# Low parts on VectorE, and weight sums beside the output projection, in the MLP of a two-layer hybrid encoder

## The chip, the cores and the metric

One core of one Trainium2 chip runs the whole program. The time is that of one execution on the device in microseconds; the number that stands for a kernel is the median of several executions. The profile is of one execution, whose own time is given beside its span.

Five engines work side by side: PE multiplies matrices and accumulates in PSUM, DVE, ACT and POOL work element by element, SP issues most DMA transfers. Each runs its own list of instructions in order, and waits where an operand is not there yet or a buffer is not free yet.

## The reference

A trunk of two layers on x of 1024 positions by 1024 features, all in float32. Layer 0 mixes by chunked attention, layer 1 by a gated DeltaNet; each is followed by the same kind of MLP, which is what the change touches.

```python
def rmsnorm(x, w):
    return x * rsqrt(mean(x * x, axis=-1) + EPS) * w

def squared_relu_mlp(h, w_up, w_down):          # w_up 1024 x 4096, w_down 4096 x 1024
    return jnp.square(jax.nn.relu(h @ w_up)) @ w_down

for i in range(2):
    x = x + mixer_i(rmsnorm(x, mixer_norm_i))   # attention, then DeltaNet; each ends in a projection w_o
    x = x + squared_relu_mlp(rmsnorm(x, mlp_norm[i]), w_up[i], w_down[i])
return rmsnorm(x, final_norm)
```

## The kernel before

**Precision.** A float32 product is made of three matmuls in a shorter format: high·high, high·low and low·high. The high part of an operand is a copy in that format (`high`, L1018, on ACT); the low part is the operand less its high part (`low`, L1011: on POOL by L1013 if the argument `pool` is set, else on DVE by L1015). So whatever is multiplied needs one operation on ACT and one on DVE or POOL first.

**Blocks.** After each mixer comes a block: its output projection (`out_proj`, L962), the up projection (`up`, L1149), the down projection. Activations lie transposed: features along the partitions, the 1024 positions in two halves of 512, called h = 0 and 1. The up projection is done in 16 units of 256 outputs, n = 0 to 15. A unit is a 2 x 2 block product by a scheme with seven products in place of eight: `block_product` (L1003) is one of the seven, 12 matmuls of 128 x 128 by 128 x 512. The scheme multiplies sums of the operands' blocks:

- sums of activations t1, t2, t3, t4, made once per block. `prep_up` (L473) makes them tile by tile as the output projection delivers x (L506, L511, L514 for the last four tiles). `finish` (in it) splits each of the sixteen tiles into high and low with `put`, sums the squares over the features on PE (the column sums, L333, of `ssum`, which L427 adds up), takes the reciprocal root on DVE in small steps (`inv_rms2`, L294 to L308, ending in `ry`), and spreads it over the partitions with PE (`row_bcast`, L347) and ACT (L349) into R.
- sums of weights S1, S2, S3 and s4, made for each unit. `up_weights` (L1031) loads two raw panels (L1036, buffers `wraw`, two of them in turn), makes four sums on POOL (L1021, L1024; the fourth is written over a quarter of the raw panel) and splits all into high and low. The first panel's parts are called w0, the second's w1; the second raw buffer comes free for the next unit's load when the low part of w1 is made. `first_up_weights` (L1108) does the same for unit 0, in buffers of its own, beside the output projection.

**Results of a unit.** A unit's products are added on DVE (L1161, L1198), scaled by R (L1163) and squared through a relu on ACT (L1164). `combine` (L1074) makes from them the sums that the down projection multiplies, four differences `c` of 128 x 512 per unit (`sub`, by `psub` on POOL), splits them (high on ACT, low on DVE at L1086) and stores them with SP (`gt<-c`, L1087). The down projection loads them again; L1458 adds its first products to x.

**Order.** The code around the change is written in the order of each engine's list: nothing is moved by a scheduler on PE, DVE, ACT and POOL, and SP's transfers follow. Generators give the steps: `out_proj` steps `weights` (which is `first_up_weights`) once for every tile of the projection, (m, h) in the order of L962, and `finish` at its end; `up` steps `finish`, and `more` and `rest` (which are `up_weights` of the next unit) between the products. In unit 0 the products come in the order: A11, A12 (added to the first on DVE), s4·22, s2·t2, s1·t1, s3·t3, 22·t4. In the later units they come as A11, s1·t1, s2·t2, A12, s3·t3, s4·22, 22·t4.

Of the kernel before, what the change touches and what calls it, by code (L numbers as in the profile page):

```python
# [12 lines left out]
ALU = mybir.AluOpType  # L13
# [195 lines left out]
class Trunk:  # L209
# [263 lines left out]
    def prep_up(self, xs, which, pool, xpool, spill):  # L473
# [44 lines left out]
        def put(t, j, pool):  # L518
            hi, lo = ops[t][j]
            self.high(hi, diffs[t][j])  # L520
            self.low(lo, diffs[t][j], hi, pool)

        def finish():
            hp = self.hi_lo()
            for t, (b, h) in {"t2": (0, 0), "t1": (4, 0), "t3": (0, 1), "t4": (4, 1)}.items():
                ops[t] = [hp[b + j][h] for j in range(4)]
            put("t2", 0, True)
            put("t2", 1, True)
            yield
            put("t2", 2, True)  # L530
            put("t1", 0, True)
            yield
            put("t2", 3, False)
            for j in range(1, 4):
                put("t1", j, True)
            yield
            r = self.inv_rms2(sums)
            next(r)
            for j in range(4):
                put("t3", j, j == 3)  # L540
                next(r, None)
                next(r, None)
            yield
            for j in range(4):
                put("t4", j, j > 1)
                next(r, None)
                next(r, None)
            for _ in r:
                pass
            yield  # L550
            R = self.new_R()
            for h in range(2):
                self.row_bcast(self.got[:, 4 * h : 4 * h + 4], R[:, h * HB : (h + 1) * HB], (self.aux, self.sqt)[h])
            yield R

        return ops, tile_done, finish()
# [405 lines left out]
    def out_proj(self, w, rhs, xs, done, finish, weights):  # L962
# [11 lines left out]
        for m, h in order:  # L974
            if h == 0 and m in self.started:
                ps = self.started[m][0]
            else:
                ps = self.bank()
                self.products(ps, *panels[m], rhs, h)
            if m < KT - 1:  # L980
                beside(2 + (m in (1, 2)))
            elif h == 0:
                beside(2)
            nc.vector.tensor_tensor(
                xs[m][:, h * HB : (h + 1) * HB], ps, xs[m][:, h * HB : (h + 1) * HB], ALU.add)
            if h == 0 and 2 <= m + 1 < KT:
                panels[m + 1] = self.load_w(w[m + 1])
            if (m, h) == (KT - 2, 1):
                beside(2)
            if (m, h) == (KT - 1, 0):  # L990
                last = done(m)
                next(last)
                beside(8)
            elif h == 1 and m < KT - 1:
                todo.append(done(m))
            next(weights, None)
        next(finish)
        next(last)
# [32 lines left out]
    def up_weights(self, i, n, ap, A):  # L1031
# [17 lines left out]
        self.padd(S1, a21, a22)  # L1049
        self.psub(S2, S1, a11)  # L1050
        yield

# [6 lines left out]
        self.high(A["s2"][0], S2)  # L1059
        self.psub(S3, a11, a21)  # L1060
        self.psub(a21, a12, S2)
        yield
# [11 lines left out]
    def combine(self, n, g, mp, gt):  # L1074
# [4 lines left out]
        def sub(z, x, y):  # L1079
            self.psub(t[z][:, HB:], x, y)  # L1080

# [25 lines left out]

    def first_up_weights(self, i, ap, ex, A):  # L1108

# [30 lines left out]
        self.low(A["s3"][1], S3, A["s3"][0], True)  # L1140
        for _ in range(5):
            yield
        w1 = [self.wp.tile([P, KT, P], F32R, name=self.nm("w" + z), tag="w" + z) for z in ("hi", "lo")]
        A["s4"], A["22"] = ([z[:, 4 * m : 4 * m + 4] for z in w1] for m in range(2))
        self.high(w1[0], raw[1])
        self.low(w1[1], raw[1], w1[0], True)
        yield

    def up(self, i, ops, ap, mp, pp, gr, gt, finish, A, tail):  # L1149

# [18 lines left out]
        for n in range(last + 1):  # L1169
            nxt, more = {}, iter(())  # L1170
            if n < last:
                more = self.up_weights(i, n + 1, ap, nxt)
# [29 lines left out]
            if n == 0:  # L1202
                next(finish)
                self.block_product(X, A["12"], ops["21"], True, True)
                add("p1", X)
                next(more)
                V = self.bank()
                self.block_product(V, A["s4"], ops["22"], True, True)
                next(finish)
                self.block_product(Y, A["s2"], ops["t2"], False, False)  # L1210
                copied("u2", Y)
                add("u2", V)
                next(more)
                self.block_product(Z, A["s1"], ops["t1"], True, True)
                copied("z5", Z)
                add("u2", Z)
                next(finish)
                next(more)
                self.block_product(Y, A["s3"], ops["t3"], False, False)
                add("z5", Y)  # L1220
                R = next(finish)
                next(more)
# [333 lines left out]
    def block(self, i, rhs, x, w, which, after, done=None, ahead=iter(()), norm=None):  # L1556
# [5 lines left out]
        with tc.tile_pool(name=f"xa{i}", bufs=1) as xa, tc.tile_pool(name=f"xb{i}", bufs=1) as xb, \  # L1562
# [7 lines left out]
            A = {}  # L1570
            first = self.first_up_weights(i, hx, ex, A)
            B = [{n: [None, None] for n in NAMES} for _ in range(2)]
# [21 lines left out]
            with tc.manual_schedule(engines=ENG):  # L1594
                self.out_proj(w, rhs, xs, tile_done, finish, first)
                sums = self.up(i, ops, hx, xp, yz, gr, gt, finish, A, end)
                next(end)
                self.down(i, hx, yz, got["xs"], chain(sums, late()), gr, gt, B, (got["A"], got["rest"]),
                          after, ahead, norm)
                if done:  # L1600
                    done(got["xs"])
# [996 lines left out]
```

## Time and profile before

| | |
|---|---|
| median of 3 runs | 2604.25 us (2602.82 to 2606.19) |
| the profiled execution | 2604.42 us |
| its span in the profile | 2602.0 us |
| mean granted clock of PE | 0.98 |
| first unit of block 0 | 563.87 to 595.38 us |
| units 1 to 14 of block 0 | from 595.38 us |
| first unit of block 1 | from 1939.42 us |

Every row of the profile names the line of the kernel, the engine, the operation, and what is written from what (`xs<-x,xs`). In a timeline a row begins with its start and its length in us; `x4` says that four like instructions follow each other; the bracket gives the idle time of the engine ahead of the row and what ended it. In a list of waits the three numbers are us in total, how often, and the longest. Names: `xs` are parts of activations (high, or low where DVE or POOL subtracts), `whi`, `wlo` the parts of raw weights, `ahi`, `alo` those of the sums of weights, `acc`, `y`, `z` accumulators in PSUM, `nt` copies of such accumulators.

### The profile page before, as it was taken

How to read it: one execution, taken by the hardware profiler on the slowest of the kernel's cores; microseconds unless marked ns; L12 is line 12 of the kernel's file. 1: busy time of each engine (PE TensorE's matmuls, PEld its weight loads, DVE VectorE, ACT ScalarE, POOL GpSimd, SP SyncE). 2: the span in 40 equal slices, each digit the busy share in tenths (PEclk: the TensorE clock that was granted, in tenths of full speed). 3: DMA queues.
4: the chain of work that ended last, by engine and by line, in shares of the span. 5: the costliest groups of instructions: out<-in, count | busy, mean ns of one | idle time of the engine just before them, and what ended most of it. 6: DMA issues, size and time to landing. Idle time of an engine off the chain costs nothing.

```text
span 2602.0 us, 36727 instructions
## 1 busy us (share of the span) xinstructions
PE 2476.6 (95%) x12638; PEld 2070.1 (80%) x12638; DVE 1925.0 (74%) x3275; ACT 1211.0 (47%) x2269; POOL 1336.2 (51%) x1112
## 2 busy tenths in 40 slices
PE   8999999999999899998888999999898999899997
PEld 6888888777888678886677788888787888688885
DVE  6665656777778778878578976675678787787887
ACT  6666667544555423234673334333335555533333
POOL 2444356536676656565464333332316666565656
PEclk9999999999999999999998999999999999999998
DMA  4222224315555876743443121123324555876642
GB/s 159 67 68 78 62 85 144 132 69 194 207 206 213 316 252 203 230 146 108 115 140 106 54 81 60 58 83 114 106 89 163 203 217 206 304 266 218 217 164 81
DMA packets 189049, 389.27 MB, mean 150 GB/s; under 512 B 54512, under 2 KB 61104, under 8 KB 188864
## 3 DMA queue, kind: packets, MB, share of 16 engines
q1 hardware_dynamic: 172592, 353.36, 40.5%
q10 hardware_dynamic: 16272, 33.58, 3.3%
q8 instruction: 99, 1.62, 0.3%
q14 instruction: 86, 0.70, 0.1%
HBM read 251.96 MB, written 126.52 MB: 145 GB/s over the span
## 4 chain that ended last, share of the span: by engine, by line
PE 59%; DVE 11%; DMA 4%; issue 3%; POOL 2%; ACT 1%; SPq 0%; DVEq 0%; ACTq 0%; POOLq 0%
PE y L1009 24%; PE z L1009 11%; PE acc L164 8%; PE acc L1009 6%; PE tp L164 3%; PE s L164 3%; DVE ft L164 2%; PE acc L280 1%; PE acc L279 1%; PE acc L278 1%; DVE fz L164 1%; DVE xs L394 1%; DMA wraw<-in_w_down_dram 1%; DVE x L1458 1%; DMA wraw<-in_w_up_dram 1%
## 5 line engine op out<-in xcount | busy, mean ns | idle before, releaser
L164 PE MATMUL acc<-xs,whi 128*128 128x512 f32 x1808 | 631.7, 413 | 8.4 <-DVE xp L164 5.2
L164 PEld LDWEIGHTS acc<-xs,whi 128*128 128x128 f32 x1808 | 333.5, 191 | 57.7 <-DVE xp L164 5.4
L164 PE MATMUL acc<-xs,wlo 128*128 128x512 f32 x896 | 368.6, 411 | 3.1 <-POOL wlo L164 3.1
L1009 PE MATMUL y<-xs,whi 128*128 128x512 f32 x1008 | 311.1, 390 | 3.5 <-DVE ssum L1161 3.5
L164 POOL TENSOR_TENSOR wlo<-wraw,whi 128x512 fp32r<-128x512 f32 x126 | 167.7, 1331 | 245.5 <-ACT whi L164 197.0
L1015 DVE TENSOR_TENSOR wlo<-wraw,whi 128x512 fp32r<-128x512 f32 (+1 forms) x180 | 202.2, 1124 | 40.1 <-ACT whi L1018 40.1
L1009 PEld LDWEIGHTS y<-xs,whi 128*128 128x128 f32 x1008 | 189.2, 188 | 43.7 <-DVE ssum L1161 4.3
L1009 PE MATMUL y<-xs,a 128*128 128x512 f32 x732 | 192.7, 400 | 23.4 <-DVE x L1458 23.3
L1024 POOL TENSOR_TENSOR s<-wraw 128x256 f32<-128x256 f32 (+1 forms) x93 | 91.9, 989 | 235.9 <-DVE a L1015 181.4
L1018 ACT ACTIVATE whi<-wraw 128x512 fp32r<-128x512 f32 (+2 forms) x191 | 146.5, 767 | 133.8 <-PE y L1009 86.1
L1009 PE MATMUL y<-xs,wlo 128*128 128x512 f32 x504 | 196.3, 389 | 0.0
L1458 DVE TENSOR_TENSOR x<-y,x 128x512 f32<-128x512 f32 x240 | 165.3, 689 | 41.1 <-PE y L1009 26.1
L1018 ACT ACTIVATE a<-s 128x256 fp32r<-128x256 f32 x122 | 63.9, 524 | 282.0 <-PE y L1009 166.5
L164 PEld LDWEIGHTS acc<-xs,wlo 128*128 128x128 f32 x896 | 171.7, 192 | 28.6 <-POOL wlo L164 4.3
L1009 PEld LDWEIGHTS y<-xs,a 128*128 128x128 f32 x732 | 139.3, 192 | 57.0 <-DVE x L1458 25.7
L1086 DVE TENSOR_TENSOR c<-c 128x512 fp32r<-128x512 f32 x128 | 151.9, 1206 | 35.7 <-POOL c L1021 34.5
L1009 PE MATMUL y<-xs,ahi 128*128 128x512 f32 x512 | 158.9, 391 | 6.1 <-DVE xs L1015 4.1
L1009 PE MATMUL acc<-xs,whi 128*128 128x512 f32 x528 | 163.6, 391 | 0.0
L164 POOL TENSOR_SCALAR pr<-pr,rs 128x640 f32<-128x640 f32 (+4 forms) x128 | 88.1, 692 | 129.3 <-DVE rs L164 96.7
L1009 PE MATMUL z<-xs,whi 128*128 128x512 f32 x480 | 149.8, 394 | 0.0
L164 POOL TENSOR_TENSOR cy<-cy,cz 128x512 f32<-128x512 f32 x48 | 69.0, 1437 | 144.6 <-DVE cz L164 122.9
L1021 POOL TENSOR_TENSOR c<-g,ssum 128x512 f32<-128x512 f32 x32 | 41.5, 1296 | 180.5 <-ACT g L1164 169.4
(330 smaller groups left out, 6378.1 us busy)
## 6 DMA issues: line engine op xcount, KB each, us to landing
gt<-c SPq DMA_DIRECT2D x128, 512.0 KB, 2.8
xs<-gt SPq DMA_DIRECT2D x256, 256.0 KB, 4.4
wraw<-in_w_up_dram SPq DMA_DIRECT2D x64, 512.0 KB, 3.4
wraw<-in_w_down_dram SPq DMA_DIRECT2D x64, 512.0 KB, 4.2
r<-gr SPq DMA_DIRECT2D x96, 256.0 KB, 3.4
wraw<-in_w_in_dram SPq DMA_DIRECT2D x32, 512.0 KB, 3.4
gr<-ssum ACTq DMA_DIRECT2D x62, 256.0 KB, 3.2
wraw<-in_w_qkv_dram SPq DMA_DIRECT2D x30, 512.0 KB, 3.3
```

The source lines that it names most:

```text
L164: return call(*args, **more)
L278: nc.tensor.matmul(ps, hi[:, k], xh, start=(k == 0), stop=False)
L279: nc.tensor.matmul(ps, hi[:, k], xl, start=False, stop=False)
L280: nc.tensor.matmul(ps, lo[:, k], xh, start=False, stop=(k == KT - 1))
L394: self.nc.vector.scalar_tensor_tensor(lo, x, w, hi.bitcast(F32), ALU.mult, ALU.subtract)
L1009: nc.tensor.matmul(ps, w[:, k], x, start=bool(first and f), stop=bool(last and e), skip_group_check=True)
L1015: self.nc.vector.tensor_tensor(lo, src, hi.bitcast(F32), ALU.subtract)
L1018: self.nc.scalar.activation(hi, src, AF.Copy)
L1021: self.nc.gpsimd.tensor_tensor(out, x, y, ALU.subtract)
L1024: self.nc.gpsimd.tensor_tensor(out, x, y, ALU.add)
L1086: nc.vector.tensor_tensor(t[z][:, HB:].bitcast(F32R), t[z][:, HB:], t[z][:, :HB], ALU.subtract)
L1458: nc.vector.tensor_tensor(x, ps, x, ALU.add)
```

## The change

It has four parts, each in both blocks.

1. `finish` makes all low parts of t1 to t4 on DVE; ten of the sixteen were on POOL. The order becomes t2, t1 (with the steps of the reciprocal root between them), t3, row broadcast, t4. The column sums come ahead of s4·22, the row broadcast ahead of s3·t3. The first two t2 tiles are split within `out_proj`, ahead of the last tile's add.
2. `first_up_weights` splits w1 one step earlier, with its low part on DVE (it was on POOL).
3. Unit 1's `up_weights` is created ahead of the projection, and its first two steps (the loads and the four sums on POOL) are taken at the end of `first_up_weights`, beside the output projection; in unit 0 its remaining steps follow. Within `up_weights` the sums S3 and the one written over the raw panel stand right behind S1 and S2.
4. `combine` makes its four differences on DVE in place of POOL.

```diff
@@ finish, in prep_up
-            put("t2", 0, True)
-            put("t2", 1, True)
-            yield
-            put("t2", 2, True)
-            put("t1", 0, True)
+            put("t2", 0, False)
+            put("t2", 1, False)
+            yield
+            put("t2", 2, False)
             yield
             put("t2", 3, False)
-            for j in range(1, 4):
-                put("t1", j, True)
             yield
             r = self.inv_rms2(sums)
             next(r)
             for j in range(4):
-                put("t3", j, j == 3)
-                next(r, None)
-                next(r, None)
-            yield
-            for j in range(4):
-                put("t4", j, j > 1)
-                next(r, None)
-                next(r, None)
+                put("t1", j, False)
+                for _ in range(3):
+                    next(r, None)
             for _ in r:
                 pass
+            yield
+            for j in range(4):
+                put("t3", j, False)
             yield
             R = self.new_R()
...
             yield R
+            for j in range(4):
+                put("t4", j, False)
+            yield
@@ out_proj
+            if (m, h) == (KT - 1, 0):
+                next(finish)
             next(weights, None)
-        next(finish)
+        next(last)
         next(last)
         next(finish)
@@ up_weights
         self.psub(S2, S1, a11)
+        self.psub(S3, a11, a21)
+        self.psub(a21, a12, S2)
         yield
...
-        self.psub(S3, a11, a21)
-        self.psub(a21, a12, S2)
@@ combine
         def sub(z, x, y):
-            self.psub(t[z][:, HB:], x, y)
+            nc.vector.tensor_tensor(t[z][:, HB:], x, y, ALU.subtract)
@@ first_up_weights(self, i, ap, ex, A, more)
-        for _ in range(5):
+        for _ in range(4):
             yield
...
-        self.low(w1[1], raw[1], w1[0], True)
-        yield
+        self.low(w1[1], raw[1], w1[0])
+        for _ in range(2):
+            next(more)
+        yield
@@ up(self, i, ops, ap, mp, pp, gr, gt, finish, A, second, tail), unit 0
-            if n < last:
+            if n == 0:
+                nxt, more = second
+            elif n < last:
                 more = self.up_weights(i, n + 1, ap, nxt)
...
-                next(more)
+                next(finish)
                 V = self.bank()
                 self.block_product(V, A["s4"], ops["22"], True, True)
-                next(finish)
                 self.block_product(Y, A["s2"], ops["t2"], False, False)
                 copied("u2", Y)
                 add("u2", V)
-                next(more)
+                next(finish)
                 self.block_product(Z, A["s1"], ops["t1"], True, True)
                 copied("z5", Z)
                 add("u2", Z)
-                next(finish)
+                R = next(finish)
                 next(more)
                 self.block_product(Y, A["s3"], ops["t3"], False, False)
                 add("z5", Y)
-                R = next(finish)
+                next(finish)
                 next(more)
```

The next lists show instructions in the order in which they are issued. Line numbers behind the change are a few higher or lower than before: L982 is the projection's add L984 of before, L1203 is L1198, L1166 is L1163, L1164 is L1161; L1080 is the new line of the difference on DVE. The numbers behind the names only tell buffers apart.

DVE's list in unit 0 before, from the first row behind the column sums (L336 reads them; `xs` here are t3 lows, `rv`, `rt`, `ry`, `ru` the steps of the reciprocal root):

```order
L336 TENSOR_SCALAR rv_6764<-aux_6755 128x8
L1015 TENSOR_TENSOR xs_6666<-x_6110,xs_6666 128x512
L294 TENSOR_SCALAR rt_6768<-rv_6764 128x8
L296 TENSOR_SCALAR ry_6769<-rt_6768 128x8
L1015 TENSOR_TENSOR xs_6668<-x_6112,xs_6668 128x512
L301 TENSOR_TENSOR ru_6770<-ry_6769 128x8
L303 SCALAR_TENSOR_TENSOR ru_6770<-ru_6770,rv_6764 128x8
```

Here the steps stand between t3 lows, and the chain goes on behind this piece between adds and t4 lows.

DVE's list in unit 0 now, from the four t3 lows (`xs_6661` to `xs_6667`) to the second unit's w0 low (`xs_6669` to `xs_6675` are t4 lows, `alo` and `wlo` belong to unit 1, `z_6721` is s1·t1, `y_6720` s3·t3):

```order
L1015 TENSOR_TENSOR xs_6661<-x_6110,xs_6661 128x512
L1015 TENSOR_TENSOR xs_6663<-x_6112,xs_6663 128x512
L1015 TENSOR_TENSOR xs_6665<-x_6114,xs_6665 128x512
L1015 TENSOR_TENSOR xs_6667<-x_6116,xs_6667 128x512
L1203 TENSOR_TENSOR nt_6807<-z_6721,nt_6807 128x512
L1203 TENSOR_TENSOR nt_6830<-y_6720,nt_6830 128x512
L1015 TENSOR_TENSOR xs_6669<-x_6118,xs_6669 128x512
L1015 TENSOR_TENSOR xs_6671<-x_6120,xs_6671 128x512
L1015 TENSOR_TENSOR xs_6673<-x_6122,xs_6673 128x512
L1015 TENSOR_TENSOR xs_6675<-t_6713,xs_6675 128x512
L1015 TENSOR_TENSOR alo_6602<-s_6598,ahi_6601 128x512
L1015 TENSOR_TENSOR wlo_6608<-wraw_6594,whi_6607 128x1024
```

The steps of the reciprocal root now stand among the t1 lows, ahead of this piece; the t4 lows stand behind the add that reads s3·t3, and the low parts for unit 1 behind them.

POOL's list in block 0 before, from the low part of unit 0's w1 on (`xs` are t2, t1, t3 and t4 lows, `s` and `wraw` the sums of unit 1):

```order
L1013 TENSOR_TENSOR wlo_6636<-wraw_6145,whi_6635 128x1024
L1013 TENSOR_TENSOR xs_6665<-x_6118,xs_6665 128x512
L1013 TENSOR_TENSOR xs_6667<-x_6120,xs_6667 128x512
L1013 TENSOR_TENSOR xs_6669<-x_6122,xs_6669 128x512
L1013 TENSOR_TENSOR xs_6673<-x_6110,xs_6673 128x512
L1013 TENSOR_TENSOR xs_6675<-x_6112,xs_6675 128x512
L1013 TENSOR_TENSOR xs_6677<-x_6114,xs_6677 128x512
L1013 TENSOR_TENSOR xs_6679<-x_6116,xs_6679 128x512
L1013 TENSOR_TENSOR xs_6672<-x_6116,xs_6672 128x512
L1024 TENSOR_TENSOR s_6800<-wraw_6740 128x512
L1021 TENSOR_TENSOR s_6801<-s_6800,wraw_6738 128x512
L1013 TENSOR_TENSOR xs_6678<-x_6122,xs_6678 128x512
```

POOL's list in block 0 now, behind the low parts of unit 0's own sums (rows with `s_6598` to `wraw_6596` are the sums of unit 1, the next four those of unit 2):

```order
L1013 TENSOR_TENSOR alo_6187<-s_6182,ahi_6186 128x512
L1013 TENSOR_TENSOR alo_6189<-s_6183,ahi_6188 128x512
L1024 TENSOR_TENSOR s_6598<-wraw_6596 128x512
L1021 TENSOR_TENSOR s_6599<-s_6598,wraw_6594 128x512
L1021 TENSOR_TENSOR s_6600<-wraw_6594,wraw_6596 128x512
L1021 TENSOR_TENSOR wraw_6596<-wraw_6594,s_6599 128x512
L1024 TENSOR_TENSOR s_6979<-wraw_6943 128x512
L1021 TENSOR_TENSOR s_6980<-s_6979,wraw_6941 128x512
L1021 TENSOR_TENSOR s_6981<-wraw_6941,wraw_6943 128x512
L1021 TENSOR_TENSOR wraw_6943<-wraw_6941,s_6980 128x512
```

The eleven low parts are gone from POOL, and the sums of unit 1 stand ahead of where those began.

DVE's list at the end of a steady unit before, from the add of a product (`g`) to the split of the differences (`c`):

```order
L1161 TENSOR_TENSOR g_6885<-z_6908,nt_6962 128x512
L1163 SCALAR_TENSOR_TENSOR g_6885<-g_6885,R_6854 128x512
L1015 TENSOR_TENSOR alo_6985<-s_6980,ahi_6984 128x512
L1163 SCALAR_TENSOR_TENSOR g_6886<-y_6907,R_6854 128x512
L1015 TENSOR_TENSOR alo_6987<-s_6981,ahi_6986 128x512
L1015 TENSOR_TENSOR wlo_6991<-wraw_6943,whi_6990 128x1024
L1086 TENSOR_TENSOR c_7058<-c_7058 128x512
L1086 TENSOR_TENSOR c_7060<-c_7060 128x512
```

The same place now:

```order
L1164 TENSOR_TENSOR g_6885<-z_6908,nt_6962 128x512
L1166 SCALAR_TENSOR_TENSOR g_6885<-g_6885,R_6833 128x512
L1015 TENSOR_TENSOR alo_6985<-s_6980,ahi_6984 128x512
L1166 SCALAR_TENSOR_TENSOR g_6886<-y_6907,R_6833 128x512
L1080 TENSOR_TENSOR c_7058<-g_6885,ssum_6884 128x512
L1080 TENSOR_TENSOR c_7060<-ssum_6884,g_6885 128x512
L1015 TENSOR_TENSOR alo_6987<-s_6981,ahi_6986 128x512
L1080 TENSOR_TENSOR c_7059<-ssum_6884,c_7058 128x512
L1080 TENSOR_TENSOR c_7061<-g_6886,c_7059 128x512
L1015 TENSOR_TENSOR wlo_6991<-wraw_6943,whi_6990 128x1024
L1086 TENSOR_TENSOR c_7058<-c_7058 128x512
L1086 TENSOR_TENSOR c_7060<-c_7060 128x512
```

Four differences (L1080) stand among the low parts, all four ahead of the w1 low.

More of the change, by code (lines that the diff above doesn't have):

```diff
@@ L539, in finish @@
             for j in range(4):
-                put("t3", j, j == 3)
-                next(r, None)
-                next(r, None)
+                put("t1", j, False)
+                for _ in range(3):
+                    next(r, None)
+            for _ in r:
+                pass
             yield
             for j in range(4):
-                put("t4", j, j > 1)
-                next(r, None)
-                next(r, None)
-            for _ in r:
-                pass
+                put("t3", j, False)
             yield
@@ L1106, in combine, with first_up_weights @@
         yield
-    def first_up_weights(self, i, ap, ex, A):
+    def first_up_weights(self, i, ap, ex, A, more):
         w0 = [ex.tile([P, KT, P], F32R, name=self.nm("w" + z), tag=f"x{n}") for n, z in enumerate(("hi", "lo"))]
@@ L1145, in first_up_weights, with up @@
         self.high(w1[0], raw[1])
-        self.low(w1[1], raw[1], w1[0], True)
+        self.low(w1[1], raw[1], w1[0])
+        for _ in range(2):
+            next(more)
         yield
-    def up(self, i, ops, ap, mp, pp, gr, gt, finish, A, tail):
+    def up(self, i, ops, ap, mp, pp, gr, gt, finish, A, second, tail):
         nc = self.nc
@@ L1570, in block @@
             A = {}
-            first = self.first_up_weights(i, hx, ex, A)
+            A1 = {}
+            more = self.up_weights(i, 1, hx, A1)
+            first = self.first_up_weights(i, hx, ex, A, more)
             B = [{n: [None, None] for n in NAMES} for _ in range(2)]
@@ L1595, in block @@
                 self.out_proj(w, rhs, xs, tile_done, finish, first)
-                sums = self.up(i, ops, hx, xp, yz, gr, gt, finish, A, end)
+                sums = self.up(i, ops, hx, xp, yz, gr, gt, finish, A, (A1, more), end)
                 next(end)
```

## The prediction

> **What bounds the kernel now.** I read four views: busy time by engine on the page, a table of PE's stretches, PE's waits within them, and the timelines of the two stretches in which PE does not run through. On the page PE is the engine that fills the span:
>
> ```profile
> PE 2476.6 (95%) x12638; PEld 2070.1 (80%) x12638; DVE 1925.0 (74%) x3275; ACT 1211.0 (47%) x2269; POOL 1336.2 (51%) x1112
> ```
>
> So work taken from POOL or given to DVE counts only where PE waits for it. The table of windows (length, PE busy, instructions, granted clock, DMA share, GB/s) tells where that is:
>
> ```profile
> 563.87:595.38 31.51, 24.88 (x118) 0.89 0.10 35
> 587.00:592.50 5.50, 3.36 (x16) 0.50 0.01 1
> 595.38:871.00 275.62, 275.62 (x1215) 1.00 0.58 216
> 871.00:900.00 29.00, 17.85 (x74) 0.94 0.94 359
> 1939.40:1970.93 31.53, 24.93 (x118) 0.89 0.09 35
> ```
>
> From 595.38 to 871 (units 1 to 14 of block 0's up projection) PE is busy all the time: nothing can be gained there, only lost. The first unit, 563.87 to 595.38, and its twin in block 1, from 1939.4, lose 6.6 us each to waits; so does the junction of up and down behind 871. PE's waits in the first unit are two:
>
> ```profile
> PE aux L347 <- DVE ry L308: 4.6, 1, 4.6
> PE y L1009 <- DVE xs L1015: 2.1, 1, 2.1
> ```
>
> **The first unit, which the change is about.** PE's timeline (start, length, line, operation), cut to its turning points:
>
> ```profile
> 563.87 0.62 PE L1009 MATMUL y<-xs,whi 128*128 128x512 f32 x2
> ...
> 572.03 1.84 PE L333 MATMUL aux<-ones,ssum 128*128 128x1 f32 x16
> 573.73 0.72 PE L1009 MATMUL y<-xs,ahi 128*128 128x512 f32 x2
> ...
> 589.14 2.04 PE L347 MATMUL aux<-ident,ry 128*128 128x128 f32 x8 [4.56 <-DVE ry L308]
> ...
> 592.52 0.71 PE L1009 MATMUL y<-xs,whi 128*128 128x512 f32 x2
> ...
> 595.38 0.61 PE L1009 MATMUL y<-xs,whi 128*128 128x512 f32 x2
> ```
>
> Three products take 572.03 − 563.87 = 8.16 us, 2.72 each; seven are 19.04. The column sums (L333) take 573.73 − 572.03 = 1.70. The row broadcast (L347) takes 592.52 − 589.14 = 3.38, but at the granted clock of 0.50 that stands in the second window, right behind the 4.56 us wait. The same eight matmuls behind a short wait take half:
>
> ```profile
> 40.76 1.13 PE L347 MATMUL po<-ident,ry 128*128 128x128 f32 x8 [0.83 <-DVE ry L308]
> 41.64 0.71 PE L164 MATMUL acc<-xs,whi 128*128 128x512 f32 x2
> ```
>
> 0.88 for eight, 1.76 for sixteen. The floor of the unit is 19.04 + 1.70 + 1.76 = 22.5 us, against 31.5: at most **9.0 us per block** can go.
>
> Why DVE is late with `ry` is shown by its rows beside POOL's, and by the same operations where POOL is still:
>
> ```profile
> 562.16 2.77 DVE L511 SCALAR_TENSOR_TENSOR x<-x,norms,x 128x512 f32<-128x512 f32 x1
> 573.36 0.68 DVE L1015 TENSOR_TENSOR xs<-t,xs 128x512 fp32r<-128x512 f32 x1
> 573.96 0.68 DVE L1198 TENSOR_TENSOR nt<-acc,nt 128x512 f32<-128x512 f32 x1
> 576.95 1.26 DVE L294 TENSOR_SCALAR rt<-rv 128x8 int32<-128x8 int32 x1
> ```
>
> ```profile
> 573.91 5.51 POOL L1013 TENSOR_TENSOR xs<-x,xs 128x512 fp32r<-128x512 f32 x4 [1.81 <-PE aux L333]
> ```
>
> ```profile
> 539.39 0.75 DVE L511 SCALAR_TENSOR_TENSOR x<-x,norms,x 128x512 f32<-128x512 f32 x1
> 2588.24 0.16 DVE L303 SCALAR_TENSOR_TENSOR ru<-ru,rv 128x2 f32<-128x2 f32 x1
> 2588.44 0.16 DVE L306 SCALAR_TENSOR_TENSOR ru<-ru 128x2 f32<-128x2 f32 x1
> ```
>
> L511 takes 2.77 beside POOL and 0.75 alone; a step of the reciprocal root 1.26 against 0.16 (one every 0.20; 2 columns there, 8 here). While POOL's lows run, a DVE operation on SBUF holds until POOL's current one ends. An add from PSUM (573.96) is not held. With the ten lows on DVE, which cost 573.96 − 573.36 = 0.60 each, POOL is idle in this unit and the small steps fall to 0.20.
>
> I follow the changed order with these prices. The column sums now stand behind the second product, 563.87 + 5.44 = 569.31. Their input is L427 of the last tile. To say when it comes I need what is newly in front of it on DVE: the w1 low (1024 wide), the two first t2 lows, and POOL's four sums for unit 1, which start when the raw weights land.
>
> ```profile
> 590.71 1.22 DVE L1015 TENSOR_TENSOR wlo<-wraw,whi 128x1024 fp32r<-128x1024 f32 x1
> 591.85 0.69 DVE L1163 SCALAR_TENSOR_TENSOR ssum<-nt,R 128x512 f32<-128x512 f32 x1
> ...
> 558.63 0.69 DVE L984 TENSOR_TENSOR x<-acc,x 128x512 f32<-128x512 f32 x1 [2.13 <-PE acc L280]
> 560.11 0.75 DVE L367 SCALAR_TENSOR_TENSOR xs<-x,norms,xs 128x512 fp32r<-128x512 f32 x1 [0.79 <-ACT xs L366]
> ```
>
> ```profile
> 549.60 0.33 SPq L1036 DMA_DIRECT2D wraw<-in_w_up_dram  x1
> ```
>
> Such a load lands 3.3 us after its issue (849.15 to 852.44 in the rows of the steady units below), here at 552.9; POOL's sums then fill 552.9 to about 559, where DVE used to wait 2.13 us for PE. DVE's 1.14 (591.85 − 590.71) for w1 and the holds push the add of 558.63 to about 559.5 if L427, whose second input is in PSUM, is not held, and to 561.2 if it is. From there: 1.48 to L367 (560.11 − 558.63), L367 and L427 1.3, three steps of the sums 2.3, two lows 1.2, the last add and its L367 1.5 to 1.8, L427 1.2: 568.4 or 570.2. So PE waits 0 or 0.9 us at the column sums; no row shows L427 beside POOL. Bounds 0 and 2.2; I take 0.4, between the two.
>
> [...]
>
> Behind the sums, DVE has L336, four t1 lows and the 0.20 steps, and `ry` is ready near 577.3; PE has three products from 569.31 + 1.70 = 571.0 and comes to L347 at 579.2. **The 4.56 us wait goes whole**, and with it the halved clock (1.62). The 2.1 wait for a t3 low goes too: behind `ry` DVE has an add and four t3 lows, five times 0.60, so they are made by 580.4, and PE wants them behind the broadcast, at 579.2 + 1.76 = 580.9.
>
> What is late next is t4. On DVE its four lows are now queued behind the add of z5 (L1198 before), which needs the s3·t3 product that ends at 583.65; add and low take 1.3 while PE wants the first low 0.45 in: PE waits about **1.1** (0.9 to 2.0 if the add is itself late). The second unit's w0 low stands behind the last t4 low, one half-width low and its own 1.14; PE, at 587.4 then, wants it at 587.9 and gets it at 588.6: **0.8** (0.3 to 1.5). Before the change POOL made the last two t4 lows, so these waits take the place of the ones removed.
>
> Sum: 9.0 − 0.4 − 1.1 − 0.8 = **6.7 us per block** (3.8 to 7.5), 13.4 for both. PE's work in the unit is only reordered; SP's queue issues the same loads in the same order up to here.
>
> **The junction.** Unit 15's last differences stood on POOL behind a sum that waits for raw weights, and DVE's add for PE's next product stood behind them:
>
> ```profile
> 896.51 1.26 POOL L1021 TENSOR_TENSOR c<-ssum,c 128x512 f32<-128x512 f32 x1
> ```
>
> ```profile
> 897.81 0.69 DVE L1086 TENSOR_TENSOR c<-c 128x512 fp32r<-128x512 f32 x1 [1.25 <-POOL c L1021]
> 898.42 0.68 DVE L1458 TENSOR_TENSOR x<-y,x 128x512 f32<-128x512 f32 x1
> ```
>
> ```profile
> 899.16 2.07 PE L1009 MATMUL y<-xs,a 128*128 128x512 f32 x4 [5.91 <-DVE x L1458]
> ```
>
> PE waits 5.91 for that add; DVE's 1.25 wait for POOL goes, as the four new subtractions (0.60 each) fit into DVE's idle time ahead of it. The rest of the 5.91 is a transfer (DMA share 0.94 in that window). I take 1.25 per block, **2.5** in all (0 to 5.2, if the add gets to go earlier still or the transfers hold it anyway).
>
> **The steady units.** Each now has four subtractions on DVE, 2.4 us, all of them ahead of the w1 low. PE never waits here, so the question is whether a loop gets longer: w1 low, then SP loads the next raw weights into its buffer, POOL sums them, DVE makes the w0 low of the next unit.
>
> ```profile
> 847.72 1.41 DVE L1015 TENSOR_TENSOR wlo<-wraw,whi 128x1024 fp32r<-128x1024 f32 x1 [0.83 <-ACT whi L1018]
> ...
> 861.17 1.22 DVE L1015 TENSOR_TENSOR wlo<-wraw,whi 128x1024 fp32r<-128x1024 f32 x1
> ```
>
> ```profile
> 849.15 0.33 SPq L1036 DMA_DIRECT2D wraw<-in_w_up_dram  x1
> 851.03 2.03 SPq L1087 DMA_DIRECT2D gt<-c  x2
> ```
>
> ```profile
> 852.44 1.41 POOL L1024 TENSOR_TENSOR s<-wraw 128x512 f32<-128x512 f32 x1 [0.29 <-DMA wraw<-in_w_up_dram]
> ```
>
> ```profile
> 862.42 0.62 PE L1009 MATMUL y<-xs,whi 128*128 128x512 f32 x2
> ```
>
> The next unit starts at 862.42 and wants the low part 0.45 later, 862.87; it is ready at 862.39. **The slack is 0.48 us.** Ahead of the w1 low come 2.4 us in place of 1.8 us of waits and holds (0.83 for ACT, the rest from POOL's differences, which are gone), so it ends about 0.6 later; some of that is made good behind it, where the c lows no longer wait for POOL. I cost the 28 units at 0.07 each: **+2** in all (0 to +11).
>
> **Sum**, against the profiled run of 2604.42 (span 2602.0 and 2.42 around it; the median of the runs is 2604.25, so nothing is to be shifted): −13.4 − 2.5 + 2 = −13.9, hence **2590.5 us**.
>
> **The rivals.** (A) The steady loop becomes the bound: the slack is used up and each of the 28 units waits 0.2 to 0.4, 5.6 to 11.2 us. For it speaks the 0.48, against it that DVE's waits for POOL's c go. 2604.4 − 15.9 + 5.6 to 11.2 = 2594 to 2600; chance 0.16. (B) Slower: the stores of c were issued 1.88 us behind the raw load (851.03 against 849.15) and would now come about 0.6 behind the w1 low; they share the DMA with it. One store of 0.52 MB at the 359 GB/s of the junction's window is 1.46 us; added to the loop with the 0.6, less 0.48, each unit loses 1.6, 28 units 44 us: 2632. It decides above 0.75 us per unit, where 28 × 0.75 = 21 eats up the gain of 15.9 and 5.2 more. Against it: a DMA share of 0.58 in the steady window. Chance 0.08. (C) The waits of the first unit only move (the column sums 2 us late behind POOL's new sums, t4 2 us late), so that the clock halves again: 2 us per block remain, 2598 to 2602; 0.08. (D) All new waits are covered: 2604.4 − 18 − 2.5 = 2584; 0.06. My forecast has 0.62.
>
> **How the numbers follow.** The measurement of this kernel tells some 0.2% (5.2 us) from no change: faster is below 2599.0, slower above 2609.6. Faster takes the forecast, D and most of A: 0.78; the same takes the rest of A, C and the slow edge of the forecast: 0.14; slower is B: 0.08. The range reaches from the floor, 2 × 9.0 and both junctions at their best (2582), to the upper end of A (2600).
>
> **What would show it.** Right: unit 1 starts about 24.8 us after the first unit; the wait L347 for `ry` is gone and the clock is 1.0 there; in its place two waits of about 1 us for L1015 lows, of t4 and of the second unit's w0. POOL's four sums run near 553 to 559. The junction's wait for the add is 1.2 shorter. Wrong: a wait of PE for a `wlo` low in every steady unit (A, or B where the raw load lands well over 3.3 us after its issue), or a wait above 2 us at L333 (C).

## The result, and the profile after

| | before | changed |
|---|---|---|
| median of 12 runs each | 2604.2 us (2599.76 to 2612.36) | 2609.36 us (2604.63 to 2611.82) |
| ratio, 95% interval | | 1.0016 (1.0008 to 1.0023) |
| span of the profiled execution | 2602.0 us | 2605.5 us |

The changed kernel is 0.16% slower, not 0.5% faster. The work moved as the change says: on the page of the changed kernel POOL has lost 240 us, DVE has gained 33, and PE's share is what it was.

```profile
PE 2484.9 (95%) x12638; PEld 2059.4 (79%) x12638; DVE 1958.4 (75%) x3425; ACT 1209.7 (46%) x2269; POOL 1096.0 (42%) x962
```

DVE took on 150 operations (64 differences and 11 low parts in each block), some 90 us at 0.60 each, and is busy only 33 us more, because its other operations are held by POOL less often: the 90 low parts `alo` of 128 x 512 alone take 61 us where they took 83.

The same table of PE's stretches as before, now from the first unit's first matmul to the second unit's, then to the end of the steady units, for both blocks:

```profile
562.76:586.95 24.19, 23.27 (x118) 1.00 0.06 23
586.95:862.00 275.05, 273.20 (x1177) 1.00 0.57 207
...
1939.68:1963.90 24.22, 23.31 (x118) 1.00 0.06 23
1963.90:2240.80 276.90, 273.84 (x1178) 1.00 0.57 206
```

The first units fell from 31.5 to 24.2 us, and PE's clock there is 1.00. But in the steady units PE is no longer busy all the time. How long a steady unit is can be read from the starts of its s1·t1 product (`z<-xs,ahi`), in the second unit and in the last, before and after:

```profile
598.10 0.61 PE L1009 MATMUL z<-xs,ahi 128*128 128x512 f32 x2
...
865.14 0.62 PE L1009 MATMUL z<-xs,ahi 128*128 128x512 f32 x2
```

```profile
590.25 0.61 PE L1009 MATMUL z<-xs,ahi 128*128 128x512 f32 x2
...
865.18 0.62 PE L1009 MATMUL z<-xs,ahi 128*128 128x512 f32 x2
```

Before, 267.04 us for 14 units, 19.07 each; after, 274.93, **19.64 each**. The 7.85 us by which the changed kernel is ahead at 590.25 (6.7 from its first unit, 1.1 from the stages before it, 562.76 against 563.87) are gone by 865.18: both kernels reach the last unit at the same time. In block 1 the same rows stand 276.84 apart (1967.15 and 2243.99), 19.77 each, where seven products of 2.72 take 19.04.

The spans differ by +3.5 us, which comes by stage from the same kind of rows: the first units −6.7 each, measured to the second unit's second product; the steady units +7.9 and +10.3; what follows the last s1·t1 product up to the end of each block's products −2.4 and −0.8; the rest, +2.0, lies in stages that the change leaves alone. These vary from kernel to kernel by more than that: between the blocks, from 722.6 to 727.6 us over all the profiles here.

### The profile page after: what moved, and what is told of

It reads as the page before. It is cut to its first block, busy times and chain, and to the rows that moved or that the text cites. A ratio compares the mean times of both kernels' runs of the same rounds, so it can differ in the third digit from the quotient of the medians.

```text
span 2605.5 us, 36618 instructions
## 1 busy us (share of the span) xinstructions
PE 2484.9 (95%) x12638; PEld 2059.4 (79%) x12638; DVE 1958.4 (75%) x3425; ACT 1209.7 (46%) x2269; POOL 1096.0 (42%) x962
## 4 chain that ended last, share of the span: by engine, by line
PE 56%; DVE 15%; issue 4%; DMA 3%; ACT 2%; POOL 1%; SPq 0%; ACTq 0%; DVEq 0%; POOLq 0%
PE y L1009 21%; PE z L1009 10%; PE acc L164 8%; PE acc L1009 7%; PE tp L164 3%; PE s L164 3%; DVE c L1086 3%; DVE ft L164 1%; PE acc L280 1%; PE acc L278 1%; PE acc L279 1%; DVE wlo L1015 1%; DVE ssum L1164 1%; DVE x L1462 1%; DVE fz L164 1%
## 5 line engine op out<-in xcount | busy, mean ns | idle before, releaser
L164 DVE CUSTOM_DVE_ANT_0 pr<-sp,bias 128x640 f32<-128x640 f32 (+4 forms) x128 | 83.8, 655 | 63.9 <-PE sp L164 62.9
```

What stands on the lines that cost most here:

```text
L164: return call(*args, **more)
```

## Where the time went: the steady unit

DVE, POOL and PE in one steady unit of the changed kernel, from the w0 low of this unit to that of the next:

```profile
724.86 1.21 DVE L1015 TENSOR_TENSOR wlo<-wraw,whi 128x1024 fp32r<-128x1024 f32 x1
...
731.70 1.22 DVE L1015 TENSOR_TENSOR wlo<-wraw,whi 128x1024 fp32r<-128x1024 f32 x1
...
737.09 0.69 DVE L1164 TENSOR_TENSOR ssum<-acc,nt 128x512 f32<-128x512 f32 x1 [2.97 <-PE acc L1009]
737.82 1.02 DVE L1166 SCALAR_TENSOR_TENSOR ssum<-ssum,R 128x512 f32<-128x512 f32 x1
738.76 1.79 DVE L1086 TENSOR_TENSOR c<-c 128x512 fp32r<-128x512 f32 x1
...
741.18 1.07 DVE L1166 SCALAR_TENSOR_TENSOR ssum<-ssum,R 128x512 f32<-128x512 f32 x1
742.17 1.78 DVE L1086 TENSOR_TENSOR c<-c 128x512 fp32r<-128x512 f32 x1
743.88 0.68 DVE L1015 TENSOR_TENSOR alo<-s,ahi 128x512 fp32r<-128x512 f32 x1
744.48 1.21 DVE L1015 TENSOR_TENSOR wlo<-wraw,whi 128x1024 fp32r<-128x1024 f32 x1
```

```profile
737.00 1.29 POOL L1024 TENSOR_TENSOR s<-wraw 128x512 f32<-128x512 f32 x1 [13.22 <-DMA wraw<-in_w_up_dram]
738.37 1.63 POOL L1021 TENSOR_TENSOR s<-s,wraw 128x512 f32<-128x512 f32 x1
739.96 1.74 POOL L1021 TENSOR_TENSOR s<-wraw,wraw 128x512 f32<-128x512 f32 x1
741.78 1.63 POOL L1021 TENSOR_TENSOR wraw<-wraw,s 128x512 f32<-128x512 f32 x1
```

```profile
745.05 0.61 PE L1009 MATMUL y<-xs,whi 128*128 128x512 f32 x2
745.74 0.50 PE L1009 MATMUL y<-xs,wlo 128*128 128x512 f32 x1
```

The reader is to see three things. DVE waits 2.97 us for the A12 product and then works without a pause to the end of the w0 low at 745.69; PE's next unit has begun at 745.05 and takes that low part as soon as it is there. So the unit is set by a **chain**: A12 product, then eight operations on DVE up to the w0 low, then PE. Four of the eight take 1.02 to 1.79 instead of 0.69, and all four lie beside POOL's four sums. The sums start when the raw panel lands (737.00), 4.1 us behind the w1 low that frees its buffer (731.70 + 1.22).

Before, the same chain ran like this, with POOL's last sum below:

```profile
854.46 0.69 DVE L1161 TENSOR_TENSOR ssum<-acc,nt 128x512 f32<-128x512 f32 x1 [1.75 <-PE acc L1009]
855.18 1.83 DVE L1163 SCALAR_TENSOR_TENSOR ssum<-ssum,R 128x512 f32<-128x512 f32 x1
856.94 1.78 DVE L1086 TENSOR_TENSOR c<-c 128x512 fp32r<-128x512 f32 x1
...
859.36 0.69 DVE L1163 SCALAR_TENSOR_TENSOR ssum<-ssum,R 128x512 f32<-128x512 f32 x1
859.97 0.69 DVE L1086 TENSOR_TENSOR c<-c 128x512 fp32r<-128x512 f32 x1
```

```profile
856.55 1.62 POOL L1021 TENSOR_TENSOR wraw<-wraw,s 128x512 f32<-128x512 f32 x1
```

There POOL was done 3.7 us into the chain (858.17 against 854.46) and the second half of it ran freely; after the change POOL is done 6.3 us into it (743.41 against 737.09). The chain takes 8.6 us (737.09 to 745.69) where it took 7.9 (854.46 to 862.39). PE leaves three products and 0.45 us for it, 8.61, from the end of one A12 product to the use of the next w0 low, and DVE takes up the product 0.2 later: 8.4 us are left, and the low part is 0.2 late. (The unit shown of before is one of the longer ones: over 13 units of block 0 the median of the chain is 7.6 us before and 8.6 after.)

That is not the whole surplus of a unit. Of the 8.4 us that the 14 units of block 0 take beyond seven products each, 5.3 lie between the starts of 22·t4 and s1·t1, where the w0 low is used, and 3.1 between those of s1·t1 and A12. The second part comes from the same chain by way of ACT:

```profile
747.05 0.63 ACT L1167 ACTIVATE g<-g 128x512 f32<-128x512 f32 x1 [3.10 <-DVE g L1166]
...
750.31 0.58 ACT L1187 ACTIVATE nt<-y 128x512 f32<-128x512 f32 x1
```

```profile
750.95 0.73 PE L1009 MATMUL y<-xs,ahi 128*128 128x512 f32 x2
```

Behind the late w0 low, DVE scales the next `g` late, ACT waits 3.10 us for it, and its copy of the A11 product (`nt<-y`), which stands behind that in ACT's list, ends at 750.89. PE begins s2·t2, which goes on in the same `y`, at 750.95. Before, the copy was done 0.65 us ahead of s2·t2 (848.17 against 848.82).

## The experiments

Each of the ten kernels was timed in five rounds beside the kernel before, on the same chip; x1 to x4, x5 to x9, and x10 with x12 ran as three groups on three chips, so across groups the ratios are to be compared. The columns: the median; the ratio to the kernel before with its 95% interval; the first unit of block 0 up to the second unit's second product, less 2.72; the mean steady unit of block 0, from the starts of the s1·t1 products of the second and the last unit.

| kernel | median us | ratio (95%) | first unit us | steady unit us |
|---|---|---|---|---|
| before | 2601.8 to 2603.3 | 1 | 31.51 | 19.07 |
| changed | 2609.36 | 1.0016 (1.0008 to 1.0023) | 24.77 | 19.64 |
| x1: differences back on POOL | 2591.39 | 0.9957 (0.9943 to 0.9970) | 24.75 | 19.17 |
| x2: before + differences on DVE | 2615.79 | 1.0052 (1.0039 to 1.0064) | 32.67 | 19.63 |
| x3: w1 low first | 2589.10 | 0.9948 (0.9936 to 0.9961) | 24.75 | 19.10 |
| x4: two differences on POOL | 2629.24 | 1.0104 (1.0090 to 1.0118) | 24.75 | 20.39 |
| x5: x3, lows on POOL | 2587.27 | 0.9937 (0.9924 to 0.9949) | 25.74 | 19.10 |
| x6: second pair split early | 2583.85 | 0.9923 (0.9909 to 0.9937) | 24.76 | 19.08 |
| x8: x3 and x6 | 2585.37 | 0.9925 (0.9913 to 0.9937) | 24.78 | 19.07 |
| x9: before + lows on DVE | 2590.67 | 0.9947 (0.9934 to 0.9959) | 25.82 | 19.04 |
| x10: before + late load | 2658.07 | 1.0213 (1.0199 to 1.0227) | 32.57 | 20.81 |
| x12: x6, t4 lows early | 2583.51 | 0.9927 (0.9915 to 0.9940) | 24.63 | 19.04 |

**x1: which part loses.** `combine` as before, the other parts as changed.

```diff
-            nc.vector.tensor_tensor(t[z][:, HB:], x, y, ALU.subtract)
+            self.psub(t[z][:, HB:], x, y)
```

> The changed kernel with only part 4 undone: the four differences of each unit are on POOL again. Theory T1 (the four differences stand ahead of the w1 low on DVE, so the next raw panel is loaded later and POOL's four sums fall beside DVE's chain that ends in the next w0 low, and hold it): the steady unit falls from 19.62 to 19.04 us, the first units keep their 7 us each, the junction's gain goes: about 2590 to 2593. Theory T2 (DVE simply has too much to do in a unit, wherever it stands): the same. Rival (the first units' gain is given back later whatever stands in the steady units): 2603 to 2605.

It came out at 2591.39. The steady unit is 19.04 in most units (the second and third take 19.8 and 19.3), the first unit keeps its gain, and the part behind the last s1·t1 product is as long as before (349.3 us in block 0). The forecast of the first unit holds; the loss belongs to part 4.

**x2: part 4 alone.** The opposite edit in the kernel before.

```diff
-            self.psub(t[z][:, HB:], x, y)
+            nc.vector.tensor_tensor(t[z][:, HB:], x, y, ALU.subtract)
```

> The kernel before with only part 4: the differences on DVE, all else as before. T1 and T2: steady units of about 19.6 us, 28 x 0.58 = 16 us lost, 3 won at the junctions: about 2617. Rival (the loss needs the first unit's new order, which starts the loop late): 2601 to 2605, steady units 19.04.

2615.79, with steady units of 19.63. So part 4 costs the same without the rest of the change, and the rival by which the loss needs the new first unit falls.

**x3: is it the amount of work on DVE, or its place?** Only the order is changed: the w1 low stands ahead of the second pair of differences.

```diff
+                next(rest, None)
                 next(sums)
                 self.block_product(Z, A["s1"], ops["t1"], True, False)
-                next(rest, None)
```

> The changed kernel with the w1 low moved ahead of the second pair of differences, so two of the four stand behind it; DVE's work is the same. T1: the load starts about 0.95 us earlier in the unit, POOL's sums overlap DVE's chain less, unit 19.1 to 19.3: 2595 to 2601. T2: unit 19.6, 2609.

2589.10 us, better than its range, and 19.04 from the fourth unit on, with the very same operations on DVE. It is the place. DVE's chain in x3, and POOL's last sum:

```profile
714.71 0.69 DVE L1164 TENSOR_TENSOR ssum<-acc,nt 128x512 f32<-128x512 f32 x1 [3.02 <-PE acc L1009]
715.43 1.52 DVE L1166 SCALAR_TENSOR_TENSOR ssum<-ssum,R 128x512 f32<-128x512 f32 x1
716.88 1.78 DVE L1086 TENSOR_TENSOR c<-c 128x512 fp32r<-128x512 f32 x1
...
719.90 0.69 DVE L1086 TENSOR_TENSOR c<-c 128x512 fp32r<-128x512 f32 x1
...
721.11 1.22 DVE L1015 TENSOR_TENSOR wlo<-wraw,whi 128x1024 fp32r<-128x1024 f32 x1
```

```profile
716.49 1.62 POOL L1021 TENSOR_TENSOR wraw<-wraw,s 128x512 f32<-128x512 f32 x1
```

POOL is done 3.4 us into the chain, and the second half is free again, as it was before the change.

**x4: less work on DVE, but POOL beside the w1 low.** The second pair of differences goes to POOL.

```diff
         def sub(z, x, y):
+            if z in ("t2", "t4"):
+                self.psub(t[z][:, HB:], x, y)
+                return
             nc.vector.tensor_tensor(t[z][:, HB:], x, y, ALU.subtract)
```

> The changed kernel with the second pair of differences (t2, t4) on POOL, the first pair on DVE: 1.2 us less on DVE in a unit, and the w1 low 1.2 us less late, or held by up to 1.1 by POOL's differences. T1: unit 19.1 to 19.3, 2595 to 2601. T2: half of the surplus gone, unit 19.3, about 2601.

Both theories expected a gain, and it lost some 20 us more. The rows say why: POOL's differences hold the w1 low itself (2.31 us against 1.22), so the load, which waits for it, comes later still, and POOL's sums reach the end of the chain (a low part of 1.78 against 0.68).

```profile
734.96 1.79 DVE L1015 TENSOR_TENSOR alo<-s,ahi 128x512 fp32r<-128x512 f32 x1
736.68 2.31 DVE L1015 TENSOR_TENSOR wlo<-wraw,whi 128x1024 fp32r<-128x1024 f32 x1
...
748.79 1.78 DVE L1015 TENSOR_TENSOR alo<-s,ahi 128x512 fp32r<-128x512 f32 x1
```

The place fits T1, which had allowed for a hold of the w1 low, but not for what follows from it. T2 has no room for a loss with less work.

**x10: a late load alone, with no work moved to DVE.** In the kernel before, the w1 low is put behind the low part of the first difference.

```diff
                 self.block_product(Z, A["s1"], ops["t1"], True, False)
-                next(rest, None)
                 beside(1, lambda: next(more, None), lambda: copied("z5", Z))
                 next(sums)
+                next(rest, None)
```

> The kernel before, differences on POOL and all else as it was, with one move: the w1 low of each unit stands behind the low part of the first difference (c of t1), so the load of the next raw panel starts 2 to 3.5 us later; DVE's and POOL's work is the same. If it is the late load that costs (it brings POOL's sums beside DVE's chain that ends in the w0 low), the steady unit is 19.4 to 20.4 us: 2613 to 2642. If the late load is harmless and DVE's extra work in the changed kernel is what costs: 19.04, 2602 to 2606.

2658.07: the direction is T1's, and the loss is larger than its upper end, since the hold falls on three operations at the very end of the chain, the w0 low among them, and PE waits in every unit:

```profile
756.12 1.79 DVE L1086 TENSOR_TENSOR c<-c 128x512 fp32r<-128x512 f32 x1
757.84 1.78 DVE L1015 TENSOR_TENSOR alo<-s,ahi 128x512 fp32r<-128x512 f32 x1
759.54 2.30 DVE L1015 TENSOR_TENSOR wlo<-wraw,whi 128x1024 fp32r<-128x1024 f32 x1
```

```profile
761.90 0.50 PE L1009 MATMUL y<-xs,wlo 128*128 128x512 f32 x1 [1.33 <-DVE wlo L1015]
```

**x6: shorten the chain and leave the load late.** The low parts of the second pair go into the time in which DVE waits for A12. In all but the last unit the steps of `combine` are taken two at a time, after s1·t1 and after s2·t2; the w1 low stays where the change put it.

```diff
                 beside(1, lambda: next(more, None), lambda: copied("z5", Z))
                 next(sums)
+                if n < last:
+                    next(sums)
...
                 copied("u2", Y)
                 next(sums)
+                if n < last:
+                    next(sums)
...
                 beside(2, lambda: next(more, None), lambda: put(2 * n, 0, X, keep["p1"]))
-                next(sums)
+                if n == last:
+                    next(sums)
```

> The changed kernel with the low parts of the second pair of differences (c of t2 and t4) ahead of the add of the A12 product on DVE, in the 3 us in which DVE waits for that product; the w1 low and so the load of the raw panel stand where the change put them. T1a (DVE's chain from the A12 product to the next w0 low is what sets the unit, and POOL's sums only lengthen it): 2 x 1.7 us go from the chain, steady unit 19.04, 2591 to 2595. T1b (the loop w1 low, load, POOL's sums, low part of S1, w0 low sets the unit): nothing of that loop is shorter, the unit stays at 19.5 or more, 2606 or more.

2583.85, better than its range, with steady units of 19.04 from the fourth on; PE's only wait for a low part in them is 0.3 us in the second unit. Behind the w0 low, the w1 low and the load come as late as in the changed kernel (6.9 us to the end of the w1 low, 4.1 more to POOL's first sum, in both), so the loop through the raw panel (T1b) is not what sets the unit; DVE's chain is, and POOL's sums lengthen it. x8, both edits, came out at 2585.37, a little below its range, and adds nothing beyond x6:

> Both the w1 low first (x3) and the second pair's low parts early (x6). T1a: units are at 19.04 already with x3, except the second and third, which lost 0.7 and 0.2: up to 0.9 us per block to win, 2587 to 2589.

**x9 and x5: what the first unit's gain needs.** x9 is the kernel before with nothing but the ten low parts of `finish` on DVE (every `True` in its `put` calls turned to `False`, and `j == 3` and `j > 1` too); x5 is x3 with those ten back on POOL in the new order.

> The kernel before with one thing of part 1 alone: the ten low parts of t1 to t4 on DVE, everything in the old order, differences on POOL, unit 1's sums in unit 0, w1 low on POOL. If the holds by POOL are the reason for the first unit's waits: ry is ready before PE comes to L347, the 4.6 and 2.1 us waits and the halved clock go, first unit 22.5 to 25: 2602 minus 13 to 18 = 2584 to 2589, without the loss in the steady units. If the new order is needed: first unit 28 or more, 2595 to 2602.

> The kernel with the w1 low first (x3, 2589.1 us), but with the ten low parts of t1 to t4 back on POOL; the new order of finish stays. If POOL's lows hold DVE's small steps (the prediction's reason for the first unit), the wait at L347 for ry comes back by 2 to 4 us per block and the first unit is 27 to 29 us instead of 24.75: 2593 to 2598. If the new order alone makes the gain: 24.7 and 2589.

x9 gave 2590.67 and a first unit of 25.82, between its two cases: the small steps of the reciprocal root take 0.15 to 0.17 each, and of the 4.6 us wait 1.7 is left:

```profile
PE aux L347 <- DVE ry L308: 1.7, 1, 1.7
PE y L1009 <- DVE nt L1198: 0.4, 1, 0.4
```

But x5 gave 25.74, where 27 to 29 was expected: with the rest of the change (the new order of `finish`, and parts 2 and 3) the root is ready in time although POOL makes the lows: PE shows no wait at L347. Either half gives some 5.7 us of the 6.7; they do not add up. The prediction counted the move to DVE as the cause; it is one of two halves, each of which takes most of the loss away without the other. The new order was not tried without parts 2 and 3.

**x12: the wait for t4.** x6 with the t4 lows ahead of the add that reads s3·t3.

```diff
                 R = next(finish)
+                next(finish)
                 next(more)
                 self.block_product(Y, A["s3"], ops["t3"], False, False)
                 add("z5", Y)
-                next(finish)
                 next(more)
```

> x6 (2583.85 us) with the t4 lows ahead of the add that reads s3 x t3 in unit 0. If that add is what makes PE wait 0.9 us for t4, as the prediction has it, this wait goes and the first unit is 23.9 instead of 24.76: 2582 to 2583. If ACT's high parts of t4 are late instead, the wait stays or grows: 2584 or more.

The wait did not go, it grew to 1.7 us, and the first unit is 24.63:

```profile
PE y L1009 <- DVE nt L1203: 1.7, 1, 1.7
```

PE waits for the add, not for the low parts behind it: 22·t4 accumulates on the same `y` that the add reads, and no other product stands between the two, as s4·22 does in the later units. The steady units are 19.04 from the first one on, as DVE comes out of unit 0 less late: PE's wait of 0.3 us for the second unit's w0 low is gone. The median does not differ from x6's.

## Why the prediction was wrong

**Right in size: the first unit.** Predicted −6.7 us per block, measured −6.74 (31.51 to 24.77) in block 0. That it is right to 0.04 us is luck, since errors of its terms cancel, and the cause was given too narrowly (x5). In the window of the first unit the wait at L347 and the halved clock are gone and two waits stand in their place:

```profile
PE y L1009 <- DVE nt L1203: 0.9, 1, 0.9
PE y L1009 <- DVE wlo L1015: 0.3, 1, 0.3
```

They stand for the terms 1.1 and 0.8. For t4 1.1 was taken and 1.6 came: s3·t3 and 22·t4 take 7.04 us (579.91 to 586.95), where two products without a wait take 5.44. The wait in it was put down to the t4 low and is the add's own (x12). For the second unit's w0 low 0.8 was taken and 0.6 came (the first product there takes 3.30 us, 586.95 to 590.25, against 2.72). PE does not wait at the column sums, where 0.4 was taken. That term hung on whether L427, with one input in PSUM, is held beside POOL; here it is not (0.67 us, where its median is 0.68), while L367 is (1.78 against 0.75):

```profile
554.17 1.78 DVE L367 SCALAR_TENSOR_TENSOR xs<-x,norms,xs 128x512 fp32r<-128x512 f32 x1
555.88 0.67 DVE L427 TENSOR_TENSOR ssum<-ssum,sqt 128x512 f32<-128x512 f32 x1
```

```profile
553.09 2.32 POOL L1021 TENSOR_TENSOR s<-s,wraw 128x512 f32<-128x512 f32 x1
555.36 1.74 POOL L1021 TENSOR_TENSOR s<-wraw,wraw 128x512 f32<-128x512 f32 x1
```

Part 3, POOL's sums beside the projection, cost PE nothing there: PE shows no wait from 540 to 563 us, before or after.

**The junction: the wait went, its worth is open.** −2.5 in all was predicted. DVE's 1.25 us wait for POOL's `c` is gone, the part of the blocks behind the last s1·t1 product is 2.4 and 0.8 us shorter, and in x1, without part 4, it is as long as before or longer. But x9, where the differences are on POOL and DVE still waits 1.24 us for them, has that part 2.9 us shorter in block 0 too (346.3 against 349.3), so the runs do not show how much of the 2.4 is due to part 4.

**Wrong: the steady units.** The step that failed is "I cost the 28 units at 0.07 each: +2 in all (0 to +11)". They cost 0.56 and 0.73 each, 18.2 us in all, and ate up the gain of 16.7. The mechanism is rival A's, the steady units becoming the bound, but beyond the 0.2 to 0.4 per unit that it was given; its sign, a wait of PE for a `wlo` low, is seen at 745.74 (0.2 us late). Two things were missed in that step. First, it followed the load as a dependency (w1 low, load, sums, w0 low) with 0.48 us of slack to use up; x6 shows that this loop was not the one that binds. Second, it did not ask what the later sums would stand beside. The price was on the prediction's own page, a DVE operation beside POOL takes 1.1 us more (1.26 against 0.16); it was used for the first unit and not for the 28 others. In the two units shown POOL's sums end 2.6 us later along DVE's chain, and four things make that up. The w1 low ends 0.7 us later behind the w0 low, which was forecast at 0.6 (6.16 us before, 842.97 to 849.13; 6.85 after, 726.07 to 732.92). The raw panel lands 0.8 later behind the w1 low (3.31 us, 849.13 to 852.44; 4.08, 732.92 to 737.00). The four sums take 0.7 longer beside a busy DVE (5.73 and 6.41). And the add of A12 comes 0.5 sooner behind the w0 low (11.49 and 11.02). Over the steady units of the two blocks the medians of that end are 4.3 and 3.7 us into the chain before, 6.3 and 6.4 after.

Rival B (stores of c that delay the load) is borne out in its kind, though not in its price of 1.6 us per unit. The stores now follow the load at 0.6 us, as B said; before it was 1.88 (849.15 and 851.03):

```profile
732.95 0.33 SPq L1036 DMA_DIRECT2D wraw<-in_w_up_dram  x1
733.55 0.93 SPq L1087 DMA_DIRECT2D gt<-c  x2
```

From the end of the w1 low to POOL's first sum the median over the steady units of a block is 3.3 to 3.4 us before and 4.1 after. It is 4.0 to 4.2 in all six kernels in which the stores follow at 0.6 us (changed, x2, x4, x6, x10, x12) and 3.3 to 3.4 in the six in which they follow at 1.9 (before, x1, x3, x5, x8, x9). In these kernels the place of the stores always moves together with that of the w1 low, so that the stores are what delays the landing is inferred, not shown. A late landing is no loss where DVE's chain is short enough (x6, 4.1 us and units of 19.08); it costs by moving POOL's sums along the chain. No run has it without a later w1 low, but one unit of the kernel before does: its w1 low is on time, its panel lands 4.71 us later,

```profile
815.65 1.30 POOL L1024 TENSOR_TENSOR s<-wraw 128x512 f32<-128x512 f32 x1 [1.69 <-DMA wraw<-in_w_up_dram]
```

its chain takes 8.42 us, and PE loses 0.5 us behind it at the same two places, which are all that the steady units of that block lose.

## What to carry to other kernels

Where two engines hold each other up, a transfer's due time is not enough: what starts when it lands must be placed too. Here an operation that came 0.7 us later, with stores that moved up behind the load, was enough to bring POOL's sums beside a critical chain. When work is moved onto an engine, look at what it is put in front of: here two differences ahead of the one operation that frees a buffer cost more than the engine's whole extra load (x3 has the same load and no loss). And two edits that remove the same wait don't add up: test each alone before counting it as the cause.

## What the runs showed of the hardware that was not expected

The hold between DVE and POOL is paid by both: a sum of POOL that takes 1.29 us beside a waiting DVE (737.00; 1.30 in the kernel before, at 853.93) takes 1.63 to 1.74 beside a busy one in the three rows behind 737.00, and a 1024-wide low part on DVE takes 2.30 in x10 instead of 1.22. How much a kernel loses depends on how many operations of the critical chain lie beside them: the same four sums per unit cost the kernel before 0.5 us in one unit and nothing in the others, and in x10 they made each unit 1.7 us longer (20.81 against 19.07), with no operation added.

The fastest kernels here, x6, x8 and x12, are at 0.9923 to 0.9927 of the kernel before (the intervals reach from 0.9909 to 0.9940), with the change's first unit and without its loss. Whether a third buffer for the raw panels would take POOL's sums out of the chain was not tried.
